# Linear attention's chunks with four tiles of its output gate between them, its result transposed after the fourth and fifth product of the first mixing, two first weights in pages

## The chip, the core and the metric

The program runs on one core of a Trainium2 chip. The metric is device time in microseconds (us) of one execution, from start to end of the whole layer; lower is better. Engines of the core run side by side and each works its own queue of instructions in order: TensorE (PE, matmuls and transposes), VectorE (DVE), ScalarE (ACT), GpSimd (POOL) and SyncE (SP, which here only issues transfers).

## What is computed

One layer of a streaming encoder on 1024 tokens of width 1024 in float32: four token mixers read one projection of the normed stream, each is mapped to the model's width, weighed by a gate and added up; a gated feed-forward block follows. The change lies in the fourth mixer, gated linear attention (4 heads, 64 key and 128 value columns each, chunks of 64 tokens), and in the step that maps a mixer's result to the model's width.

```python
def gla_mixer(q, k, v, g_lr, og, w_g2, b_g, o_norm):
    ...
    q_in = qc * jnp.exp(bcum)
    k_in = kc * jnp.exp(-bcum)
    k_st = kc * jnp.exp(b_last - bcum)
    tri = jnp.tril(jnp.ones((CHUNK, CHUNK), dtype=bool))
    att = jnp.where(tri, jnp.einsum('cbhtd,cbhsd->cbhts', q_in, k_in), 0.0)
    o_intra = jnp.einsum('cbhts,cbhsv->cbhtv', att, vc)
    ...
    def step(state, inp):
        q_c, k_c, v_c, d_c = inp
        o_c = jnp.einsum('bhtd,bhdv->bhtv', q_c, state)
        state = d_c[..., None] * state + jnp.einsum('bhtd,bhtv->bhdv', k_c, v_c)
        return state, o_c
    ...
    o = rms_norm(o, o_norm.reshape(GLA_HEADS, GLA_DV)).reshape(bsz, seq, GLA_VW)
    return o.astype(dt) * jax.nn.silu(og)

# in reference():
        o = jnp.stack([o_a, o_b, o_c, o_d], axis=2)
        br = jnp.einsum('bskc,kcd->bskd', o, w_branch[l])
        g = jax.nn.sigmoid(gate).reshape(bsz, seq, N_BRANCH, D_MODEL)
        mixed = jnp.sum(g * br, axis=2) @ w_out[l]
```

## The kernel before

**Exactness and tiles.** A float32 product is made of three passes in a faster format: each operand is split into a high and a low part (`split`: ACT copies the high part, DVE subtracts it to get the low one), and PE multiplies high by high, high by low and low by high. So `fm` and `tm` issue three matmuls for each block of 128 inner columns. A page is a tile of 128 partitions by 1024 numbers. Weights come through three small rings: `wr` (raw, as loaded by SP, 2 buffers), `wh` and `wl` (high and low, 3 buffers each). A raw buffer is loaded again once the split of its content has been issued and is done; a split buffer is written again once its matmuls are done. Accumulators in PSUM are also rings: `ps` has 3 buffers of 1024 columns, `p1` has 2 of 512.

**Linear attention, `gla()`.** Two pairs of heads (p = 0, 1), 8 blocks of 128 tokens, that is 2 chunks each (i). `factors()` has earlier stored six pages for each pair in DRAM: the decayed queries and keys, and `qb0`, `qb1`, which hold the queries of one head with zeros in place of the other. `gla()` loads them again as `gl` (12 pages, some of them early), then `vd`, the values, 4 pages. `within(p, i)` multiplies keys by queries into one `ps` buffer, and DVE masks the result into `att`. `across(p, i)` multiplies queries by the running state, `att` by the values, and keys by the values for the next state (`po`, a `p1` buffer); DVE updates the state, ACT copies the result into `od` (4 pages). The loop runs `within` two steps ahead of `across`. These products are plain float32 matmuls, which the trace shows as two rows for each call.

**The output gate, `gla_out_gate`.** For each of 8 token tiles: 24 matmuls of 512 columns with the weights `wog`, then Silu on ACT into `og`. In the kernel before, tiles 0 to 3 are called ahead of the loop and tiles 4 to 7 after it; the tile scheduler moves the first `within` steps between them. After the loop `norm` works on each page of `od`: Square on ACT (`sq`), a sum on DVE (L811), two small operations on POOL (`rsqrt`, L284 and L285), a multiplication on DVE (L815). `og` is multiplied by `o_norm` (DVE, L827), and `finish()` multiplies `od` by `og` (DVE, 8 pieces of 512 columns, L835) and transposes `od` on PE (32 transposes into 4 `ps` buffers, L846), copies them (`odt`, ACT) and stores them for a later mixing.

**Mixing, `mixing(k)`.** `o` holds the split result of mixer k, transposed (8 pages, from `load_o`, which loads `oraw` and splits it). For each of 8 blocks m of 128 output columns: load a weight (`wr`, 128 by 512) and the gate (`g`), split the weight, 24 matmuls into one `ps` buffer, and a DVE multiplication of that by `g` into `acc` (L893, called the evacuation of m below). Mixing 0 follows `gla()` at once. `bg` is a queue of steps that are put between (`tick`): the norms in `gla_out_gate`, then `finish()` and the loads of the next `o` (`load_o(1, h)`) between the blocks m.

The order of instructions on each engine in this part is the tile scheduler's: it is decided when the program is built and fixed in each queue. Each engine's queue is strictly in order, and so a waiting instruction holds up all behind it. In the listings below a name such as `ps_763_5420` is a buffer's name with its number, and "x2" are two instructions alike.

Of the kernel before, what the change touches and what calls it, by code (L numbers as in the profile page):

```python
# [11 lines left out]
F32R = mybir.dt.float32r  # L12
I32 = mybir.dt.int32
AF = mybir.ActivationFunctionType
# [3 lines left out]
P = 128  # L18
# [59 lines left out]
class Trunk:  # L78
# [155 lines left out]
        return prev  # L234

    SPEC = {"wb": (4, P, 4)}

    def pre(self, name, idx):

# [408 lines left out]
    def factors(self):  # L648
# [14 lines left out]
        ps = self.psum()  # L663
# [28 lines left out]
        for p in range(2):  # L692
# [35 lines left out]
            ps = self.psum()  # L728
            for i in range(NT):
                nc.tensor.transpose(ps[:, i * P:(i + 1) * P], ks2[:, i * P:(i + 1) * P], self.ident)  # L730
            qb = [self.page("qb") for _ in range(2)]
            for h in range(2):
                r, z = slice(h * 64, h * 64 + 64), slice(64 - h * 64, 128 - h * 64)
                nc.gpsimd.memset(qb[h][z, :], 0.0)
                nc.vector.tensor_copy(out=qb[h][r, :], in_=b[r, :])
                nc.gpsimd.dma_start(out=self.glo[p][3 + h], in_=qb[h])
            yield
            kt = self.page("kt")
            nc.scalar.copy(out=kt, in_=ps)
# [6 lines left out]
    def gla(self):  # L746
# [13 lines left out]
            qs, ki, ks, qb0, qb1, kt = (self.gl[p][j] for j in range(6))  # L760
            io[p] = qs, ki, ks, (qb0, qb1), kt, self.dec2[p]
        vd = [self.fetched_page(self.vds[j], "vd") for j in range(4)]
        self.gla_out_gate(range(0, 4), og, 0)

        od = [[self.page("od") for _ in range(2)] for p in range(2)]

        def within(p, i):
            qs, ki, ks, qb, kt, dec2 = io[p]
            tok = slice(i * P, (i + 1) * P)
            pa = self.psum()  # L770
            for h in range(2):
                nc.tensor.matmul(pa[:, h * P:(h + 1) * P], ki[:, tok], qb[h][:, tok], start=True, stop=True)
            for h in range(2):
                nc.tensor.matmul(pa[:, 256 + h * P:256 + (h + 1) * P], ks[:, tok], qb[h][:, tok], start=True, stop=True)
            t = att[2 * p + i % 2]
            nc.vector.copy_predicated(out=t, mask=self.tri, data=pa[:, 0:256])
            t3 = t.rearrange("p (h t) -> p h t", h=2)
            nc.vector.tensor_copy(out=t3[0:64, :, 64:128], in_=pa[0:64, 256:512].rearrange("p (h t) -> p h t", h=2)[:, :, 64:128])

        def across(p, i):  # L780
            qs, ki, ks, qb, kt, dec2 = io[p]
# [14 lines left out]
            nc.scalar.copy(out=od[p][i // 4][:, (i % 4) * 256:(i % 4) * 256 + 256], in_=po[:, 0:256])  # L796

        seq = [(p, i) for i in range(NT) for p in range(2)]
        within(*seq[0])
        within(*seq[1])  # L800
        for j, it in enumerate(seq):
            if j + 2 < len(seq):
                within(*seq[j + 2])
            across(*it)

        def norm(p, j):
# [14 lines left out]
        for h in range(4):  # L821
            for _ in self.load_o(0, h):
                pass
        self.gla_out_gate(range(4, 8), og, 2)
        for j in range(4):
            o3 = og[j].rearrange("p (b c) -> p b c", b=2)
            nc.vector.tensor_mul(out=o3, in0=o3, in1=go[:, 0:512].unsqueeze(1).to_broadcast([P, 2, 512]))  # L827
# [9 lines left out]
        def finish():  # L837
            for p in range(2):
                for j in range(2):
                    gate(p, j)  # L840
                    yield
            for p in range(2):
                for h in range(2):
                    ps = self.psum()
                    for i in range(NT):
                        nc.tensor.transpose(ps[:, i * P:(i + 1) * P], od[p][i // 4][:, (i % 4) * 256 + h * P:(i % 4) * 256 + (h + 1) * P], self.ident)  # L846
                    yield
                    o = self.page("odt")
                    nc.scalar.copy(out=o, in_=ps)
                    nc.gpsimd.dma_start(out=self.spill[3][2 * p + h], in_=o)  # L850
        self.bg.append(finish())

    def gla_out_gate(self, tiles_, og, n):
        for i in tiles_:
# [14 lines left out]
    def mixing(self, k, last=False, then=None):  # L869

        nc, a = self.nc, self.a
        o, self.o = self.o, []
        self.pre("wb", 8 * k)
        if then is not None:
            self.bg.extend(self.load_o(then, h) for h in range(4))

        def fetch(m):
            g = self.page("g")
            nc.sync.dma_start(out=g, in_=self.fmo[16 + 8 * k + m])
            return g  # L880

        nxt = fetch(0)
        for m in range(8):
            g = nxt
            if m + 1 < 8:
                self.pre("wb", 8 * k + m + 1)
                nxt = fetch(m + 1)
            self.tick(2)
            ps = self.psum()
            self.fm(ps, self.w("wb", 8 * k + m), o)  # L890
            if self.acc[m] is None:
                self.acc[m] = self.page("acc")
                nc.vector.tensor_mul(out=self.acc[m], in0=ps, in1=g)  # L893
            else:
                nc.vector.tensor_mul(out=g, in0=ps, in1=g)
                nc.vector.tensor_add(out=self.acc[m], in0=self.acc[m], in1=g)
            if last:
                nc.gpsimd.dma_start(out=self.accs[m], in_=self.acc[m])
# [61 lines left out]
    def latent(self):  # L960
# [7 lines left out]
        for i in range(NT):  # L968
            ps = self.psum1()
            self.tm(ps[:, 0:336], self.hrows(i), w)  # L970
            nc.scalar.copy(out=q_at(i, 0, 336), in_=ps[:, 0:336])
        w = self.weights(a["wc"][1], 8, 336, 3)
        sk, sq = self.small(8), self.small(8)
        junk = self.page("junk")
        for i in range(NT):
# [621 lines left out]
    def run(self):  # L1597
# [18 lines left out]
        with ExitStack() as e1:  # L1616
            self.psp = e1.enter_context(tc.tile_pool(name="psum", **big))
            with ExitStack() as e2:
# [2 lines left out]
                self.hl = hp.tile([P, 8, S], F32R, name="hl")  # L1621
                self.columns(self.ranks(self.gmlp()))
                self.o = []
                self.gla()
                for h in range(4):
                    self.dump(f"oa{h}", self.spill[0][h])
                    self.dump(f"ob{h}", self.spill[1][h])
                self.mixing(0, then=1)
                self.drain()
                for h in range(4):  # L1630
                    self.dump(f"od{h}", self.spill[3][h])
# [113 lines left out]
```

## Time and profile before

| | |
|---|---|
| median of 3 runs | 1917.24 us (1915.26 to 1917.99) |
| profiled execution, its own time | 1917.36 us |
| its span, first to last instruction | 1915.6 us |
| PE busy | 1871.1 us (98%), 9000 matmuls recorded |
| DVE / ACT / POOL busy | 65% / 45% / 11% |
| chain that ended last | PE 85%, DVE 6%, ACT, DMA, POOL and issue 2% each |
| mean granted clock of TensorE | 0.997 |

PE is busy nearly all the time, and the chain of work that ended last runs mostly through it. So a change can gain by less work on PE or by fewer of its few waits, and lose by a new wait. A profile row of a matmul states when it started and how long it took; matmuls overlap, so that the distance between starts is what one costs. The part that the change touches lies between 600 and 740 us.

### The profile page before, as it was taken

Reading aid. Unit: us, or ns where it says so; the run is one execution under the profiler, and the core shown is the slowest. Engines: PE = TensorE matmul, PEld = TensorE weight load, DVE = VectorE, ACT = ScalarE, POOL = GpSimd, SP = SyncE. Lnnn points to the kernel's source line nnn. Section 1 sums busy time; section 2 is a strip of 40 time slices with the busy share of each in tenths; the row PEclk is TensorE's granted clock in tenths of the full one; section 3 lists DMA queues with packets and bytes.
Section 4 is the critical chain, followed back from the end, with each engine's and each line's share of the span. In section 5 each row is a group of like instructions: output and inputs, shape, how many; then the busy total and the mean of one; then the engine's idle time right before and its main releaser. Section 6 shows DMA issues by size and latency. Waiting matters only on the chain.

```text
span 1915.6 us, 23556 instructions
## 1 busy us (share of the span) xinstructions
PE 1871.1 (98%) x9000; PEld 1562.5 (82%) x9000; DVE 1254.6 (65%) x1752; ACT 861.4 (45%) x1304; POOL 205.9 (11%) x357
## 2 busy tenths in 40 slices
PE   7999999999999999999999999999999999999998
PEld 6988888887887878988788788788888888888887
DVE  5757676664773557436888872687777777774652
ACT  5433465535453221242777633364444444442431
POOL 2000000010110020021122200300000000000101
PEclk9999999999999999999999999999999999999999
DMA  6123344372556335245000353213333323686651
GB/s 220 50 88 132 132 151 153 137 254 99 204 214 231 115 118 206 67 134 177 16 23 29 144 205 130 99 45 131 111 110 110 113 107 115 229 311 212 254 186 44
DMA packets 88289, 268.60 MB, mean 140 GB/s; under 512 B 9488, under 2 KB 15392, under 8 KB 88176
## 3 DMA queue, kind: packets, MB, share of 16 engines
q1 hardware_dynamic: 58896, 174.68, 26.9%
q0 software_dynamic: 21664, 78.45, 10.3%
q10 hardware_dynamic: 7616, 13.96, 2.3%
q8 instruction: 71, 1.16, 0.2%
q14 instruction: 42, 0.34, 0.1%
HBM read 186.78 MB, written 80.28 MB: 139 GB/s over the span
## 4 chain that ended last, share of the span: by engine, by line
PE 85%; DVE 6%; issue 2%; ACT 2%; DMA 2%; POOL 2%; SPq 0%; DVEq 0%; ACTq 0%; POOLq 0%
PE bk L167 22%; PE ps L167 16%; PE bk L1533 12%; PE p L277 9%; PE ps L268 7%; PE p L167 6%; PE ps L277 2%; PE ps L1081 2%; PE po L1132 2%; PE p L1266 2%; PE pp L1117 1%; POOL sm L285 1%; DVE ang L953 1%; DVE wl L123 1%; DMA gl<-gl 1%
## 5 line engine op out<-in xcount | busy, mean ns | idle before, releaser
L1533 PE MATMUL bk<-dh,g 128*128 128x512 f32 x704 | 217.1, 389 | 0.2 <-DVE q L1544 0.2
L167 PE MATMUL bk<-q,wh 128*128 128x512 f32 x704 | 216.7, 389 | 0.0
L122 ACT CAST wh<-t 128x1024 fp32r<-128x1024 f32 x85 | 89.5, 1053 | 273.4 <-PE bk L167 123.2
L123 DVE TENSOR_TENSOR wl<-wr,wh 128x1024 fp32r<-128x1024 f32 (+7 forms) x107 | 103.4, 968 | 117.9 <-ACT wh L122 116.9
L167 PE MATMUL ps<-S,wh 128*128 128x512 f32 x560 | 173.2, 390 | 1.3 <-ACT zb L216 1.3
L1533 PEld LDWEIGHTS bk<-dh,g 128*128 128x128 f32 x704 | 132.2, 188 | 28.1 <-DVE q L1544 0.6
L167 PEld LDWEIGHTS bk<-q,wh 128*128 128x128 f32 x704 | 132.2, 188 | 27.4
L122 ACT CAST wh<-wr 128x1024 fp32r<-128x1024 f32 (+7 forms) x107 | 90.4, 847 | 136.1 <-PE ps L268 67.5
L268 PE MATMUL ps<-o,wh 128*128 128x512 f32 x512 | 139.9, 394 | 3.8 <-ACT o L122 1.5
L1533 PE MATMUL bk<-dl,g 128*128 128x512 f32 x352 | 137.0, 389 | 0.0
L167 PE MATMUL bk<-q,wl 128*128 128x512 f32 x352 | 136.9, 389 | 0.0
L167 PEld LDWEIGHTS ps<-S,wh 128*128 128x128 f32 x560 | 104.8, 188 | 23.5 <-ACT zb L216 2.0
L123 DVE TENSOR_TENSOR wl<-t,wh 128x1024 fp32r<-128x1024 f32 x85 | 103.8, 1221 | 28.8 <-ACT wh L122 28.7
L268 PEld LDWEIGHTS ps<-o,wh 128*128 128x128 f32 x512 | 95.6, 189 | 25.9 <-DVE o L123 2.8
L167 PE MATMUL ps<-S,wl 128*128 128x512 f32 x280 | 109.0, 389 | 0.0
L167 PE MATMUL bk<-S,wh 128*128 128x512 f32 x304 | 93.6, 389 | 0.0
L123 DVE TENSOR_TENSOR dl<-dr,dh 128x1024 fp32r<-128x1024 f32 x44 | 53.7, 1221 | 45.5 <-ACT dh L122 38.7
L268 PE MATMUL ps<-o,wl 128*128 128x512 f32 x256 | 79.4, 393 | 3.0 <-DVE wl L123 3.0
L167 PEld LDWEIGHTS bk<-q,wl 128*128 128x128 f32 x352 | 66.1, 188 | 13.7
L1533 PEld LDWEIGHTS bk<-dl,g 128*128 128x128 f32 x352 | 66.1, 188 | 13.6
L167 PE MATMUL p<-hh,wh 128*128 128x512 f32 x184 | 72.5, 394 | 0.4 <-ACT za L206 0.4
L167 PE MATMUL p<-hh,wl 128*128 128x512 f32 x184 | 71.9, 391 | 0.9 <-DVE wl L123 0.9
(459 smaller groups left out, 4414.4 us busy)
## 6 DMA issues: line engine op xcount, KB each, us to landing
wr<-in_wf SPq DMA_DIRECT2D x48, 512.0 KB, 4.2
wr<-in_up SPq DMA_DIRECT2D x44, 512.0 KB, 3.6
dr<-in_down SPq DMA_DIRECT2D x44, 512.0 KB, 5.2
g<-fm SPq DMA_DIRECT2D x32, 512.0 KB, 5.8
fm<-za POOLq DMA_DIRECT2D x22, 512.0 KB, 2.9
fm<-zb POOLq DMA_DIRECT2D x22, 512.0 KB, 2.9
ga<-fy POOLq DMA_DIRECT2D x22, 512.0 KB, 2.9
gb<-fy POOLq DMA_DIRECT2D x22, 512.0 KB, 2.9
```

Source lines behind the costliest of these rows:

```text
L122: self.nc.scalar.copy(out=hi, in_=src)
L123: self.nc.vector.tensor_sub(out=lo, in0=src, in1=hi.bitcast(F32))
L167: self.nc.tensor.matmul(ps, l[:, c], r, start=first and k == 0 and j == 0, stop=last and k == 3 and j == 2, skip_group_check=True)
L268: self.nc.tensor.matmul(ps[:, h * 512:(h + 1) * 512], lhs, rhs[:, h * 512:(h + 1) * 512], start=first and k == 0 and j == 0, stop=last and ...
L277: self.nc.tensor.matmul(ps, lhs, rhs, start=first and k == 0 and j == 0, stop=last and k == K - 1 and j == 2)
L285: nc.gpsimd.tensor_tensor(out=r, in0=t, in1=self.mhalf[:, 0:w], op=ALU.pow)
L953: nc.vector.scalar_tensor_tensor(out=ang, in0=t, scalar=-c, in1=ang, op0=ALU.mult, op1=ALU.add)
L1081: nc.tensor.matmul(ps[:, off + c0:off + c1], l[:, q0], r[:, c0:c1], start=jj == 0, stop=jj == 2)
L1117: nc.tensor.transpose(pp[:, at:at + P], probs[u][j][0][:, kb * P:(kb + 1) * P], self.ident)
L1132: nc.tensor.matmul(po[:, c], vs[2 * m + kk][:, head * P:(head + 1) * P], ptt[:, z * 512 + kk * 256:z * 512 + kk * 256 + c.stop - c.start], ...
L1266: self.nc.tensor.matmul(ps, l, x, start=k == 0 and j == 0, stop=k == K - 1 and j == 2)
L1533: nc.tensor.matmul(ps, l, r[:, halves[c]], start=first and n == 0 and j == 0, stop=last and n == len(gs) - 1 and j == 2)
```

## The change

1. `factors()` writes the queries in another layout: each page now holds both heads of 4 token blocks side by side. It takes four DVE copies and four POOL memsets of half the size in place of two and two.
2. `within()` makes one matmul of 256 columns for both heads in place of two of 128, and one of 128 columns with 64 weight columns in place of two of 128 by 128.
3. The output gate's tiles 2 to 5 are issued in groups of six matmuls between the steps of the loop, into `ps` buffers; tiles 0 and 1 stay ahead of the loop, 6 and 7 follow it. In `gla()` SP's queue now has the order in which the code issues its loads.
4. The weights of the first block of mixing 0 and of mixing 3 are loaded and split in pages of their own (`pre_page`), not in the rings. All later weights of mixing 0 thereby move one place in the rings.
5. The transposes of `od` (`turned`) are taken out of `finish()` and go into `bg` behind the four loads of the next `o`.

```diff
+    def pre_page(self, idx):
+        raw, t = self.page("pwr")[:, 0:512], self.page("pwt", F32R)
+        self.nc.sync.dma_start(out=raw, in_=self.a["wb"][idx])
+        self.split(raw, t[:, 0:512], t[:, 512:1024])
+        self.fetched["wb", idx] = [(t[:, j * P:(j + 1) * P], t[:, 512 + j * P:512 + (j + 1) * P]) for j in range(4)]
...
-            qb = [self.page("qb") for _ in range(2)]
-            for h in range(2):
-                r, z = slice(h * 64, h * 64 + 64), slice(64 - h * 64, 128 - h * 64)
-                nc.gpsimd.memset(qb[h][z, :], 0.0)
-                nc.vector.tensor_copy(out=qb[h][r, :], in_=b[r, :])
-                nc.gpsimd.dma_start(out=self.glo[p][3 + h], in_=qb[h])
+            for n in range(2):
+                qb = self.page("qb")
+                q4 = qb.rearrange("p (i h t) -> p i h t", h=2, t=P)
+                for h in range(2):
+                    r, z = slice(h * 64, h * 64 + 64), slice(64 - h * 64, 128 - h * 64)
+                    nc.gpsimd.memset(q4[z, :, h, :], 0.0)
+                    nc.vector.tensor_copy(out=q4[r, :, h, :], in_=b[r, n * 512:(n + 1) * 512].rearrange("p (i t) -> p i t", t=P))
+                nc.gpsimd.dma_start(out=self.glo[p][3 + n], in_=qb)
...
-        self.gla_out_gate(range(0, 4), og, 0)
+        self.gla_out_gate(range(0, 2), og, 0)
...
-            for h in range(2):
-                nc.tensor.matmul(pa[:, h * P:(h + 1) * P], ki[:, tok], qb[h][:, tok], start=True, stop=True)
-            for h in range(2):
-                nc.tensor.matmul(pa[:, 256 + h * P:256 + (h + 1) * P], ks[:, tok], qb[h][:, tok], start=True, stop=True)
+            q = qb[i // 4][:, (i % 4) * 256:(i % 4) * 256 + 256]
+            nc.tensor.matmul(pa[:, 0:256], ki[:, tok], q, start=True, stop=True)
+            nc.tensor.matmul(pa[0:64, 256:384], ks[:, i * P:i * P + 64], q.rearrange("p (h t) -> p h t", h=2)[:, :, 64:128], start=True, stop=True)
...
+        def parts():
+            for i in range(2, 6):
+                ps, l = self.psum()[:, 0:512], self.hrows(i)
+                for c in range(0, 8, 2):
+                    self.tm(ps, l[c:c + 2], self.wog[c:c + 2], first=c == 0, last=c == 6)
+                    if c < 6:
+                        yield
+                nc.scalar.activation(out=og[i // 2][:, (i % 2) * 512:(i % 2) * 512 + 512], in_=ps, func=AF.Silu)
+                yield
+        fill = parts()
...
             if j + 2 < len(seq):
                 within(*seq[j + 2])
+            next(fill, None)
             across(*it)
...
-        self.gla_out_gate(range(4, 8), og, 2)
+        self.pre_page(0)
+        self.gla_out_gate(range(6, 8), og, 4)
...
+        def turned():
             for p in range(2):
                 for h in range(2):
                     ps = self.psum()
...
-        self.pre("wb", 8 * k)
+        if ("wb", 8 * k) not in self.fetched:
+            self.pre("wb", 8 * k)
         if then is not None:
-            self.bg.extend(self.load_o(then, h) for h in range(4))
+            self.bg.extend(self.load_o(then[0], h) for h in range(4))
+            self.bg.append(then[1])
...
+        self.pre_page(24)
...
-                self.gla()
+                with self.tc.manual_schedule(engines={mybir.EngineType.SP}):
+                    turned = self.gla()
...
-                self.mixing(0, then=1)
+                self.mixing(0, then=(1, turned))
```

How the queues change is shown at two places. **The end of the norms.** Before, DVE's queue has these instructions up to the first evacuation of mixing 0, L893, the last row here (L815 is a norm's multiplication, L827 `og` by `o_norm`, L835 `od` by `og`, L123 the low part of a weight):

```order
L815 TENSOR_TENSOR od_662_4891<-od_662_4891,sm_722_5250 128x1024
L815 TENSOR_TENSOR od_663_4892<-od_663_4892,sm_727_5285 128x1024
L827 TENSOR_TENSOR og_643_4760<-og_643_4760,go_639_4755 128x1024
L123 TENSOR_TENSOR wl_730_5295<-wr_728_5293,wh_729_5294 128x512
L123 TENSOR_TENSOR wl_734_5303<-wr_732_5301,wh_733_5302 128x512
L835 TENSOR_TENSOR od_661_4890<-od_661_4890,og_643_4760 128x512
L835 TENSOR_TENSOR od_662_4891<-od_662_4891,og_640_4757 128x512
L835 TENSOR_TENSOR od_662_4891<-od_662_4891,og_641_4758 128x512
L835 TENSOR_TENSOR od_663_4892<-od_663_4892,og_642_4759 128x512
L835 TENSOR_TENSOR od_663_4892<-od_663_4892,og_643_4760 128x512
L123 TENSOR_TENSOR wl_740_5342<-wr_738_5340,wh_739_5341 128x512
L893 TENSOR_TENSOR acc_737_5338<-ps_736_5313,g_731_5299 128x1024
```

In the changed kernel DVE's queue has there (L834 is a norm's sum; L838, L851 and L859 are its multiplication, `og` by `o_norm` and `od` by `og`; L922 is the evacuation of block m0 out of `ps_735`):

```order
L838 TENSOR_TENSOR od_658_4847<-od_658_4847,sm_716_5215 128x1024
L838 TENSOR_TENSOR od_659_4848<-od_659_4848,sm_720_5224 128x1024
L834 TENSOR_REDUCE sm_723_5256<-sq_722_5254 128x8
L851 TENSOR_TENSOR og_643_4770<-og_643_4770,go_639_4765 128x1024
L838 TENSOR_TENSOR od_660_4849<-od_660_4849,sm_725_5259 128x1024
L834 TENSOR_REDUCE sm_727_5265<-sq_726_5263 128x8
L859 TENSOR_TENSOR od_658_4847<-od_658_4847,og_640_4767 128x512
L838 TENSOR_TENSOR od_661_4850<-od_661_4850,sm_729_5268 128x1024
L859 TENSOR_TENSOR od_658_4847<-od_658_4847,og_641_4768 128x512
L859 TENSOR_TENSOR od_659_4848<-od_659_4848,og_642_4769 128x512
L859 TENSOR_TENSOR od_659_4848<-od_659_4848,og_643_4770 128x512
L922 TENSOR_TENSOR acc_736_5316<-ps_735_5291,g_730_5277 128x1024
```

In both the evacuation stands behind the last norm. In the changed kernel the weights' low parts come ahead of all four norms, two sums ahead of the first row here, and the four products with `og` directly ahead of the evacuation. PE's queue in the changed kernel, in the third block of mixing 0 (`ps_751` is block m2, `ps_763` is m3; m0 was `ps_735` and m1 `ps_741`):

```order
L275 MATMUL ps_751_5373<-o_699_5157,wh_738_5319 128x512 x2
L275 MATMUL ps_751_5373<-o_700_5158,wh_738_5319 128x512 x2
L275 MATMUL ps_763_5420<-o_699_5157,wh_744_5358 128x512 x2
L275 MATMUL ps_763_5420<-o_700_5158,wh_744_5358 128x512
L275 MATMUL ps_751_5373<-o_699_5157,wl_739_5320 128x512 x2
L275 MATMUL ps_751_5373<-o_702_5163,wh_738_5319 128x512 x2
L275 MATMUL ps_751_5373<-o_703_5164,wh_738_5319 128x512 x2
L275 MATMUL ps_751_5373<-o_702_5163,wl_739_5320 128x512 x2
```

Before, all 24 matmuls of a block stand together from m2 on, with transposes between m1 and m2:

```order
L268 MATMUL ps_742_5352<-o_706_5145,wh_733_5302 128x512 x2
L268 MATMUL ps_742_5352<-o_707_5146,wh_733_5302 128x512 x2
L268 MATMUL ps_742_5352<-o_706_5145,wl_734_5303 128x512 x2
L846 MATMUL ps_748_5387<-cst_72,od_661_4890 128x128 x2
L846 MATMUL ps_750_5399<-cst_72,od_660_4889 128x128 x4
L846 MATMUL ps_750_5399<-cst_72,od_661_4890 128x128 x4
L268 MATMUL ps_751_5408<-o_697_5127,wh_739_5341 128x512 x2
L268 MATMUL ps_751_5408<-o_698_5128,wh_739_5341 128x512 x2
```

So after four matmuls of m2, PE's queue now has three of m3, whose `ps` buffer is that of m0; before, blocks m0 and m1 were mixed in this way.

**Around the evacuation of m3.** Before, DVE's queue (`acc_762` is the evacuation of m3, `acc_773` that of m4):

```order
L123 TENSOR_TENSOR wl_765_5496<-wr_763_5494,wh_764_5495 128x512
L893 TENSOR_TENSOR acc_762_5492<-ps_761_5467,g_747_5385 128x1024
L123 TENSOR_TENSOR wl_776_5542<-wr_774_5540,wh_775_5541 128x512
L123 TENSOR_TENSOR o_770_5508<-oraw_768_5505,o_769_5507 128x1024
L893 TENSOR_TENSOR acc_773_5538<-ps_772_5513,g_756_5441 128x1024
```

In the changed kernel (`acc_764` is the evacuation of m3, `wl_778` is the low part of the weight of m6, the `o` pages are those of mixing 1):

```order
L123 TENSOR_TENSOR wl_767_5449<-wr_765_5447,wh_766_5448 128x512
L123 TENSOR_TENSOR wl_778_5509<-wr_776_5507,wh_777_5508 128x512
L123 TENSOR_TENSOR o_758_5409<-oraw_750_5371,o_757_5408 128x1024
L123 TENSOR_TENSOR o_761_5415<-oraw_759_5412,o_760_5414 128x1024
L922 TENSOR_TENSOR acc_764_5445<-ps_763_5420,g_746_5363 128x1024
```

The evacuation of m3 now stands behind two weights and two pages of the next `o`. SP's queue before:

```order
L131 DMA wr_774_5540<-in_wb 128x512
L879 DMA g_756_5441<-fm20_119 128x1024
L131 DMA wr_786_5587<-in_wb 128x512
L879 DMA g_766_5500<-fm21_120 128x1024
L545 DMA oraw_768_5505<-spill1_0_87 128x1024
L131 DMA wr_799_5680<-in_wb 128x512
L545 DMA oraw_771_5511<-spill1_1_88 128x1024
```

SP's queue in the changed kernel:

```order
L131 DMA wr_776_5507<-in_wb 128x512
L552 DMA oraw_750_5371<-spill1_1_88 128x1024
L908 DMA g_756_5406<-fm20_119 128x1024
L131 DMA wr_786_5566<-in_wb 128x512
L131 DMA wr_798_5658<-in_wb 128x512
L552 DMA oraw_759_5412<-spill1_2_89 128x1024
L552 DMA oraw_762_5418<-spill1_3_90 128x1024
```

The load `oraw_759`, from which `o_761` is made, now stands behind `wr_798`, whose raw buffer is that of `wr_776`, the weight that `wl_778` is made of. On PE the transposes into `ps_771` and `ps_773` now stand directly behind m3, and m4 (`ps_774`) behind these, in the buffer of m3.

## Rows read from the trace of the kernel before

**Rows 1.** Waits of PE, 612 to 700 us: total, times, longest.

```profile
PE ps L268 <- DVE wl L123: 3.0, 1, 3.0
PE p L787 <- issue: 1.4, 1, 1.4
PE ps L774 <- DMA gl<-gl: 1.0, 1, 1.0
PE ps L772 <- DVE att L778: 0.8, 1, 0.8
PE ps L772 <- DMA gl<-gl: 0.5, 1, 0.5
PE p L787 <- ACT od L796: 0.4, 1, 0.4
```

**Rows 2.** Timeline of PE in one step of the loop: start, duration, instructions.

```profile
644.00 0.61 PE L772 MATMUL ps<-gl,gl 128*128 128x128 f32 x4
...
644.88 0.60 PE L787 MATMUL p<-state,gl 128*128 128x256 f32 x2
...
646.20 0.61 PE L772 MATMUL ps<-gl,gl 128*128 128x128 f32 x4
```

**Rows 3.** Chain that ended last, the gate's last three tiles: start, length.

```profile
664.19 16.38 PE p L277 x72
```

**Rows 4.** Windows of PE: window, length, busy (instructions), granted clock, DMA share, GB/s.

```profile
691.48:694.21 2.73, 2.73 (x7) 0.50 0.59 188
...
614.00:623.00 9.00, 6.62 (x53) 1.00 1.02 411
```

**Rows 5.** Timeline of PE at the start of mixing 0.

```profile
691.48 1.22 PE L268 MATMUL ps<-o,wl 128*128 128x512 f32 x2 [3.02 <-DVE wl L123]
692.50 1.91 PE L268 MATMUL ps<-o,wh 128*128 128x512 f32 x4
694.21 0.67 PE L268 MATMUL ps<-o,wl 128*128 128x512 f32 x2
```

**Rows 6.** Timeline of ACT in the norms: start, duration of the whole row.

```profile
670.20 2.00 ACT L809 ACTIVATE sq<-od 128x1024 f32<-128x1024 f32 x2
...
682.98 1.13 ACT L122 CAST wh<-wr 128x512 fp32r<-128x512 f32 x2
```

**Rows 7.** Timeline of DVE in the norms.

```profile
671.29 2.35 DVE L811 TENSOR_REDUCE sm<-sq 128x8 f32<-128x1024 f32 x2 [3.35 <-ACT sq L809]
674.59 1.22 DVE L815 TENSOR_TENSOR od<-od,sm 128x1024 f32<-128x1024 f32 x1 [0.95 <-POOL sm L285]
677.63 1.23 DVE L815 TENSOR_TENSOR od<-od,sm 128x1024 f32<-128x1024 f32 x1 [1.82 <-POOL sm L285]
...
679.91 1.89 DVE L835 TENSOR_TENSOR od<-od,og 128x512 f32<-128x512 f32 x3
```

**Rows 8.** Timeline of POOL in the norms.

```profile
672.61 0.19 POOL L284 TENSOR_SCALAR sm<-sm 128x8 f32<-128x8 f32 x1 [62.41 <-DVE sm L811]
...
674.63 1.23 POOL L284 TENSOR_SCALAR sm<-sm 128x8 f32<-128x8 f32 x1
```

**Rows 9.** Timeline of DVE in mixing 0, a page of the next `o`.

```profile
723.59 0.68 DVE L123 TENSOR_TENSOR wl<-wr,wh 128x512 fp32r<-128x512 f32 x1
...
730.50 1.23 DVE L123 TENSOR_TENSOR o<-oraw,o 128x1024 fp32r<-128x1024 f32 x1 [1.73 <-ACT o L122]
731.65 1.22 DVE L893 TENSOR_TENSOR acc<-ps,g 128x1024 f32<-128x1024 f32 x1
```

**Rows 10.** Timeline of PE, transposes between two blocks of mixing 0.

```profile
709.08 1.03 PE L846 MATMUL ps<-cst,od 128*128 128x128 f32 x8
```

**Rows 11.** Instructions on the tile `vd`: its loads, issue to landing.

```profile
L545 SPq DMA_DIRECT2D vd<-vd x4: 319/319/448, 612.1 to 619.7; - x4
...
DMA to landing us min/median/max: 2.9/7.4/15.2
```

**Rows 12.** Instructions on the tile `oraw`, 600 to 760 us: issue to landing.

```profile
DMA to landing us min/median/max: 3.4/4.7/11.4
```

More of the change, by code (lines that the diff above doesn't have):

```diff
@@ L777, in within @@
             t3 = t.rearrange("p (h t) -> p h t", h=2)
-            nc.vector.tensor_copy(out=t3[0:64, :, 64:128], in_=pa[0:64, 256:512].rearrange("p (h t) -> p h t", h=2)[:, :, 64:128])
+            nc.vector.tensor_copy(out=t3[0:64, :, 64:128], in_=pa[0:64, 256:384].rearrange("p (h t) -> p h t", h=2))
         def across(p, i):
@@ L851, in gla @@
         self.bg.append(finish())
+        return turned()
     def gla_out_gate(self, tiles_, og, n):
```

## The prediction

> **What bounds the kernel now.** The chain that ended last was read first: it runs mostly through PE, whose matmuls follow one another without a gap nearly everywhere. So only work on PE and its waits count. PE's waits between 612 and 700 us came next [rows 1]: in the loop's region (614 to 664) they add up to 0.5 + 1.0 + 0.8 + 1.4 + 0.4 = 4.1 us, for `gl` pages, for `att`, for the state and for `od`. The longest, 3.0 us, is at the start of mixing 0, where PE stands before `wl`: on DVE that split is queued behind the last norm. Then the timelines of PE and of the engines it waits for, the windows for the clock, and for what is new the queues of the changed kernel, as the part on the change shows them.
>
> **Part 1: `within` gets narrower.** In a steady step the four calls of `within` (two rows each in the trace) start at 644.00 and the next product at 644.88, so they cost 0.88 us for 512 columns [rows 2]. A whole step takes 646.20 - 644.00 = 2.20. The new pair has 256 and 128 columns, three quarters: 0.66. I take that the time goes with the columns; that half the weight columns of the second call are left out gives nothing more. Sixteen steps by 0.22: -3.5 us. If only the number of calls counted, it would be half, 0.44 by 16 = -7.0; if the narrow call cost as much as two, 0.
>
> **Part 2: the gate's tiles between the steps.** The work is the same; a group of six matmuls costs 6 x 16.38/72 = 1.36 us [rows 3]. What could be gained are the loop's waits. But what they wait for stays late. `vd` is issued from 612.1 on and its first page lands up to 15.2 later, at 627.3 [rows 11]. PE leaves gate tile 1 at 614.0; the first steps of `within` (six at 0.66), gate tile 2 (5.5) and a wait of 1.5 to 2 for the page of `gl` that ended the old wait of 1.0 bring it to the first `across` at about 625.3: it waits some 2.0 us for `vd`, which in the kernel before gate tiles 2 and 3 covered. With some 0.4 for copies of `od` the new waits are 1.7 + 2.0 + 0.4 = 4.1, against 4.1; I book -0.2, with bounds of -3 (transfers a little earlier) and +2.
>
> **Part 3: the start of mixing 0.** Its first weight lies in a page, split while gate tile 7 runs, and its `o` pages are done: the wait of 3.0 goes: -3.0. After it the clock was at its lower level: from 691.48 to 694.21, 2.73 us, six matmuls ran at a granted clock of 0.50 [rows 4, 5], that is 1.2 GHz; at full speed they take 1.36. So another -1.4. The small waits of transposes for a copy go at one place and come at another: 0.
>
> **Part 4: what stands before PE next.** I count from C, the end of the loop. Gate tiles 6 and 7 are 48 matmuls, 10.9 us [rows 3]. Then PE has m0 (24 matmuls), m1 (24) and four of m2, and then three of m3, in the `ps` buffer of m0. So 100 matmuls after C, at C + 22.75, it needs the evacuation of m0. On DVE that stands behind the whole of the norms, and these begin late: ACT's first instruction of this stretch is the split of `wr` for m1, into a `wh` buffer that PE gives back in gate tile 7, after its sixth matmul: 30 matmuls, C + 6.8, and 0.2 to the signal. Behind it in ACT's queue wait a second cast and a Silu, about half a us each (1.13 for two casts), and the first Square, 1.0 [rows 6]: the first sum starts at about C + 9.6.
>
> From there DVE's own pace in the trace: sum to first multiplication 674.59 - 671.29 = 3.3, to the second 677.63 - 674.59 = 3.0 [rows 7]: C + 12.9 and C + 15.9. The third sum follows after 1.1 and its multiplication 3.3 later, C + 20.4; the fourth sum and multiplication likewise, C + 24.8. Then its own 1.1, three products with `og` (1.89), C + 27.8, and the evacuation, 1.2: C + 29.0. PE waits 29.0 - 22.75 = 6.3 us. POOL's first operation can make it more: it took 0.19 alone and 1.23 when a DVE multiplication ran beside it [rows 8]; in the third and fourth norm `og` by `o_norm` and a product run beside it, so up to 1.0 more each: 8.3. I take 7.0, nearer to the lower end, since the product is only half as long as a multiplication.
>
> The Trainium skill, GPSIMD Engine Reference, section 1 (Specifications), says that GpSimd shares its SBUF interface with VectorE and is held up by DVE instructions with two SBUF inputs. The trace agrees with it (0.19 against 1.23); by that rule each norm would pay, and the wait would be 8.3.
>
> **Part 5: the evacuation of m3.** Let E be the end of m3. PE has 16 transposes behind it, 1.03 for 8 [rows 10], about 2.0 us, and then m4, whose `ps` buffer is that of m3. On DVE that evacuation stands behind `wl_778` (its `wh` waits for PE's end of m3), and `o_761`. `o_761` is made of `oraw_759`, which SP issues behind `wr_798`, which waits for `wl_778`. The same chain of split, raw load, page load, its split and evacuation stands in the trace: from `wl` at 723.59 to the end of `acc` at 731.65 + 1.22, 9.3 us [rows 9]. There three buffers of `ps` gave it time. Here it starts at about E + 0.7 (the cast of `wh`) and ends at E + 10.0; PE is there at E + 2.0 and waits 8.0. A page lands in 3.4 at the least, and 4.7 in the median [rows 12], which sets the lower bound 1.3 lower, 6.7. I take 7.5.
>
> **The clock after the new waits.** A wait of 3.0 cost 1.4 after it, and in 614 to 623, with shorter waits, the clock stayed at 1.00 [rows 4]. The two new waits are longer than 3.0, so I book 1.4 for each, +2.8, with bounds of 0 and 3.4 (1.7 each). The Trainium skill, TensorE: Matmul & The Clock Gate, section "Why this matters for your kernels", advises against idle gaps between bursts of matmuls, since the clock returns to its low level. The trace agrees at 691.48; by that rule the change, which brings two such gaps, pays for both.
>
> **Edits at no cost.** The new layout of the queries moves the same number of elements in two more copies and two more memsets for each pair; it lies beside the long run of matmuls ahead of 600 us, where DVE and POOL have time; without that cover it would be four more starts, below 2 us. The page for mixing 3's first weight: that mixing waits for its `o` pages in the trace, not for a weight, so 0; a first weight has cost at most 3.0 [rows 1], so -3.0 is the other bound.
>
> **The sum.** -3.5 - 0.2 - 3.0 - 1.4 + 7.0 + 7.5 + 2.8 = +9.2 us. The profiled execution took 1917.36, 0.1 above the median: 1917.3 + 9.2 = 1926.5.
>
> **The rivals.**
> - *One wait only* (0.12). If `oraw_759` is in time, since the first wait lets the loads run ahead, or if the norms keep pace, one of the two remains: -8.1 + 7.2 + 1.4 = +0.5, 1917.8. For it speaks that a wait at m3 delays PE but not the loads before it; against it, that `wr_798` hangs on E itself, whenever that comes.
> - *No wait at all* (0.10), the other side. The evacuations come in time if the norms end 6.3 us earlier than worked out, which takes Squares that begin at C + 2 and not at C + 8.6, and if m3's evacuation hangs on no load. Then -8.1 is left: 1909.2. It decides as soon as waits and clock together stay under 4.3. For it: the Square of the first pages has its input long before C. Against it: ACT's queue, in which the cast for m1 stands ahead.
> - *The loop waits too* (0.06). If `vd` or the last `gl` page lands 2 us later, now uncovered by gate tiles, PE waits 2 more in two places and the clock falls once (1.4): 1926.5 + 3.4 = 1929.9.
>
> **How the numbers follow.** The two waits (0.72) have a range of their own: the least sum is -8.1 + 6.3 + 6.7 + 0 = +4.9, the most -8.1 + 8.3 + 8.0 + 3.4 = +11.6, so 1922 to 1929. The range reaches from the case of one wait to that of the loop, 1917.3 to 1930, and leaves out the case without waits and little else. 0.2%, 3.8 us, is about what a measurement of this kernel can tell from no change. Slower by over that: 0.72 + 0.06 = 0.78; within it, one wait: 0.12; faster: 0.10.
>
> **What the profile of the changed kernel would show.** Two waits of PE in mixing 0, some 12 us after its start and again behind the transposes after m3, each released by an evacuation on DVE and each followed by a clock of 0.5 (parts 4, 5); no wait at its start and the clock at full there (part 3); steps of the loop of 2.0 us without their gate group (part 1); a wait of about 2 us ahead of the first `across`, released by `vd` (part 2). The prediction is wrong if DVE reaches the evacuation of m0 within 22.75 us of C, or if the load behind `wr_798` lands before PE has done the transposes.

## The result and the profile after

The changed kernel took 1929.6 us in the median of 3 runs (1929.53 to 1932.64) against 1917.24: a ratio of 1.0073, 95% interval 1.0059 to 1.0086. By the ratio that is 14 us, by the medians 12.4; 9.2 had been forecast, and 1930.0 was the upper end of the range. The profiled execution is the one of 1932.64 (span 1930.9), 3 us above the other two; that part lies elsewhere, at 1105 us (below).

The page's chain that ended last, by engine:

```profile
PE 81%; issue 7%; DVE 5%; ACT 2%; POOL 2%; DMA 2%; SPq 0%; POOLq 0%; DVEq 0%; ACTq 0%
```

PE has 81% of it where it had 85%, and "issue", time for which the profile shows no cause, 7% where it had 2%. PE's waits from 600 to 760 us (total, times, longest) show where, as [rows 1] do for the kernel before:

```profile
PE ps L275 <- DVE acc L922: 14.5, 2, 7.6
PE ps L784 <- DMA gl<-gl: 0.7, 1, 0.7
PE p L797 <- issue: 0.5, 1, 0.5
PE ps L782 <- DMA gl<-gl: 0.4, 1, 0.4
...
PE p L797 <- ACT od L806: 0.2, 1, 0.2
```

The 3.0 for `wl` is gone and the loop's waits have shrunk from 4.1 to 1.8 us, but two waits for an evacuation stand in mixing 0, 14.5 us together. The windows of PE (length, busy, granted clock, DMA share, GB/s), from the first `within` to the start of mixing 0, then the two waits and what followed each of them:

```profile
613.42:683.79 70.37, 68.58 (x329) 1.00 0.33 124
...
695.74:703.36 7.62, 0.00 (x1) 0.70 0.00 0
703.36:708.99 5.63, 5.63 (x13) 0.50 0.66 234
...
718.01:724.88 6.87, 0.00 (x0) 0.84 0.95 342
724.88:729.47 4.59, 4.58 (x11) 0.50 0.28 116
```

The first wait lasts 7.62 us and the clock is at 0.50, 1.2 GHz, for 5.63 us behind it; the second 6.87, and 4.59 behind it. At 1.2 GHz half of such a stretch is lost: 2.8 and 2.3 us. The stretch ahead of mixing 0 took 70.37 us; before it was 685.83 - 613.96 = 71.87, so 1.5 were gained where 3.7 had been expected.

A step of the loop in PE's timeline, to be read against [rows 2]:

```profile
635.10 0.59 PE L782 MATMUL ps<-gl,gl 128*128 128x256 f32 x2
635.63 0.43 PE L784 MATMUL ps<-gl,gl 128*64 128x128 f32 x2
635.99 0.50 PE L284 MATMUL ps<-wh,hh 128*128 128x512 f32 x1
636.33 0.39 PE L284 MATMUL ps<-wl,hh 128*128 128x512 f32 x1
...
637.49 0.59 PE L797 MATMUL p<-state,gl 128*128 128x256 f32 x2
...
638.79 0.59 PE L782 MATMUL ps<-gl,gl 128*128 128x256 f32 x2
```

The pair of `within` runs from 635.10 to 635.99, 0.89 us, as long as the four calls before. The gate's six matmuls take 637.49 - 635.99 = 1.50 where 1.36 had been booked, and the first of them takes 0.34 to the next, the others 0.23. The whole step is 3.69 us (635.10 to 638.79); a step of before with a group would be 2.20 + 1.36 = 3.56.

The chain ahead of the first wait's end (start, length; nine of its rows):

```profile
680.44 0.61 ACT pwt L122
681.05 0.49 ACT og L884
681.55 0.96 ACT sq L832
...
682.53 1.23 DVE sm L834
...
684.12 1.67 POOL sm L292
685.87 1.24 POOL sm L291
...
690.01 1.22 DVE sm L834
...
695.39 1.14 DVE sm L834
...
701.98 1.24 DVE acc L922
```

It is that of part 4: the cast of the page, Silu, Square, the sums, each norm a turn through POOL, and the evacuation at 701.98. POOL's two small operations, four times each, are 9.7 of the 22.8 us from 680.44 to the evacuation's end, more than any other engine's share; no run here moves them to another engine. The chain ahead of the second wait's end:

```profile
715.84 0.63 ACT wh L122
...
716.49 0.70 DVE wl L123
...
717.21 0.33 SPq L131
...
717.60 3.69 DMA oraw<-spill
...
721.30 1.05 ACT o L122
...
723.52 1.23 DVE acc L922
```

That is part 5: `wh` at the end of m3, `wl`, the raw load of `wr`, the load of a page behind it in SP's queue (3.69 us), its split, and the evacuation. Two waits more were not foreseen. One is in the stage of the latent attention. The second stands at 1105 us, with 3.4 us of low clock behind it; the times of the other two runs, 3 us shorter, suggest that they do not have it:

```profile
PE sp L1296 <- DVE g L924: 1.4, 1, 1.4
```

```profile
PE ps L275 <- ACT o L122: 1.7, 1, 1.7
```

### The profile page after: what moved, and what is told of

Same layout as the page of the kernel before. It is cut to its first block, busy times and chain, and to the rows that moved or that the text cites. A ratio compares the mean times of both kernels' runs of the same rounds, so it can differ in the third digit from the quotient of the medians.

```text
span 1930.9 us, 23437 instructions
## 1 busy us (share of the span) xinstructions
PE 1874.8 (97%) x8936; PEld 1557.5 (81%) x8936; DVE 1254.8 (65%) x1756; ACT 860.1 (45%) x1304; POOL 205.1 (11%) x361
## 4 chain that ended last, share of the span: by engine, by line
PE 81%; issue 7%; DVE 5%; ACT 2%; POOL 2%; DMA 2%; SPq 0%; POOLq 0%; DVEq 0%; ACTq 0%
PE bk L167 22%; PE bk L1563 12%; PE ps L167 12%; PE ps L275 9%; PE p L284 8%; PE p L167 5%; PE ps L284 4%; PE ps L1111 2%; PE po L1162 2%; PE p L1296 1%; PE pp L1147 1%; POOL sm L292 1%; POOL sm L291 1%; DMA oraw<-spill 1%; DMA gl<-gl 1%
## 5 line engine op out<-in xcount | busy, mean ns | idle before, releaser
L123 DVE TENSOR_TENSOR wl<-wr,wh 128x1024 fp32r<-128x1024 f32 (+7 forms) x105 | 101.5, 969 | 122.4 <-ACT wh L122 121.5
L275 PE MATMUL ps<-o,wh 128*128 128x512 f32 x480 | 134.7, 401 | 16.8 <-DVE acc L922 14.5
L123 DVE TENSOR_TENSOR wl<-t,wh 128x1024 fp32r<-128x1024 f32 x85 | 103.7, 1220 | 28.7 <-ACT wh L122 28.7
L123 DVE TENSOR_TENSOR dl<-dr,dh 128x1024 fp32r<-128x1024 f32 x44 | 53.7, 1221 | 44.0 <-ACT dh L122 37.0
L275 PE MATMUL ps<-o,wl 128*128 128x512 f32 x240 | 75.5, 397 | 0.0
```

What stands on the lines that cost most here:

```text
L123: self.nc.vector.tensor_sub(out=lo, in0=src, in1=hi.bitcast(F32))
L275: self.nc.tensor.matmul(ps[:, h * 512:(h + 1) * 512], lhs, rhs[:, h * 512:(h + 1) * 512], start=first and k == 0 and j == 0, stop=last and ...
```

## The experiments

Each expectation was written before its kernel ran. Each kernel's time stands beside runs of the kernel before on the same chip (median 1917.2 in the first four, 1916.4 in the next, 1916.0 in the last), and the ratios are to these.

**x1, x2: the narrow products alone.** x1 is the kernel before with the new layout of the queries and this:

```diff
+            nc.tensor.matmul(pa[:, 0:256], ki[:, tok], q, start=True, stop=True)
+            nc.tensor.matmul(pa[0:64, 256:384], ks[:, i * P:i * P + 64], q...[:, :, 64:128], start=True, stop=True)
```

x2 differs from x1 in the second call:

```diff
+            nc.tensor.matmul(pa[:, 256:384], ks[:, tok], q...[:, :, 64:128], start=True, stop=True)
```

x1: 

> The kernel before with the new layout of the queries and the narrower pair of products in the loop alone (256 columns, and 128 columns with 64 weight columns); everything else as before. Prediction's term (time goes with the columns): a step of the loop 2.20 - 0.22 = 1.98 us, the loop 3.5 us shorter, time 1913.5 to 1914. Rival, from the trace of the changed kernel (635.10 to 635.99 for the pair, 0.89): the 64-column weights cost what the columns save, step 2.20, time 1917 within 1. Second rival: the pair costs 0.66 here, and the 0.23 more in the changed kernel is what the gate's matmuls behind it pay.

x2: 

> As the first, but the second product keeps 128 weight columns (128 partitions out, of which 64 are read). If 64 weight columns are what cost: step 1.98 us, loop 3.5 shorter, time near 1913.7. If the cost is one of calls or of the mixed widths and not of the 64 columns: the same as the first run. By the prediction's term alone both runs are alike at 1.98.

x1 took 1919.3 us, ratio 1.0012 (1.0003 to 1.0021), above both times that had been expected, part of it by the clock behind the old wait; x2 took 1915.6, 0.9996 (0.9986 to 1.0006). A step in PE's timeline of x1, and then of x2:

```profile
650.21 0.59 PE L774 MATMUL ps<-gl,gl 128*128 128x256 f32 x2
650.74 0.43 PE L776 MATMUL ps<-gl,gl 128*64 128x128 f32 x2
651.10 0.70 PE L789 MATMUL p<-state,gl 128*128 128x256 f32 x2
651.63 0.61 PE L791 MATMUL p<-vd,att 128*128 128x128 f32 x4
...
652.51 0.59 PE L774 MATMUL ps<-gl,gl 128*128 128x256 f32 x2
```

```profile
650.37 0.59 PE L774 MATMUL ps<-gl,gl 128*128 128x256 f32 x2
650.80 0.39 PE L776 MATMUL ps<-gl,gl 128*128 128x128 f32 x2
651.02 0.60 PE L789 MATMUL p<-state,gl 128*128 128x256 f32 x2
651.45 0.61 PE L791 MATMUL p<-vd,att 128*128 128x128 f32 x4
...
652.33 0.59 PE L774 MATMUL ps<-gl,gl 128*128 128x256 f32 x2
```

In x1 the pair takes 0.89 (650.21 to 651.10), and the product with the state behind it 0.53 instead of 0.44; a step is 2.30 us, longer than the 2.20 before. In x2 the pair takes 0.65 and a step 1.96. So the time does go with the columns, and the 64 weight columns cost it back, by 0.34 us in each step. The Trainium skill, TensorEngine Tiling (Array Packing), section "Key Properties", says that TensorE is drained when the tiling mode changes. The 0.34 us would fit such a change at the 64-column call, the only one that differs between x1 and x2; that this call changes the mode, or that there is a drain, no run here shows. x2 is 16 x 0.24 = 3.8 us shorter in its steps, but gave 1.6 in its median: in its profile PE waits 1.7 for `gl` and 0.9 for `att` ahead of 621.2, and the clock is low for 3.3 us behind that.

**x3: the gate's tiles between the steps alone.** The kernel before with this and with SP in code order:

```diff
-        self.gla_out_gate(range(0, 4), og, 0)
+        self.gla_out_gate(range(0, 2), og, 0)
...
+            next(fill, None)
             across(*it)
...
-        self.gla_out_gate(range(4, 8), og, 2)
+        self.gla_out_gate(range(6, 8), og, 4)
```

> The kernel before with the gate's tiles 2 to 5 between the steps of the loop and the loads of that part in code order alone; four calls in each step as before, mixing as before. Prediction's term: -0.2 us in all, work between the steps costs nothing of its own. Rival: each change from plain float32 matmuls to split ones costs 0.11 us (in the trace of before 623.40 to 623.72 is 0.32 where others are 0.227), 16 changes, +1.6, less the old loop's waits that go (4.1 to about 1.8): -0.7. The wait at the start of mixing 0 stays near 3.0 with its clock loss. Time 1915 to 1918.

It took 1922.3, ratio 1.0025 (1.0014 to 1.0036): above both expectations. Its longest wait, and a group of the gate behind four calls of 128 columns, in PE's timeline:

```profile
PE ps L268 <- DVE wl L123: 9.0, 1, 9.0
```

```profile
648.40 0.47 PE L277 MATMUL ps<-wh,hh 128*128 128x512 f32 x1
648.72 0.39 PE L277 MATMUL ps<-wl,hh 128*128 128x512 f32 x1
...
649.87 0.59 PE L787 MATMUL p<-state,gl 128*128 128x256 f32 x2
...
651.18 0.61 PE L772 MATMUL ps<-gl,gl 128*128 128x128 f32 x4
...
651.99 0.47 PE L277 MATMUL ps<-wh,hh 128*128 128x512 f32 x1
```

The wait at the start of mixing 0 has grown from 3.0 to 9.0. With two gate tiles left behind the loop, and not four, the norms have 10.9 us less cover; in the kernel before, the first two norms ran beside tiles 5 and 6 [rows 7]. The wait grew by less than 10.9, since `wl` stands behind three multiplications of norms in x3's DVE queue (it starts at 694.80) and behind four in that of before.

A group takes 1.47 here and its first matmul 0.32 to the next, but the four calls ahead of it take 0.81 (651.18 to 651.99) and not 0.88. The step is 3.59 (648.40 to 651.99), and 2.20 + 1.36 = 3.56: the change from plain to split matmuls costs some 0.03 us in a step, not the rival's 0.11. From the first `within` to the start of mixing 0 x3 takes 69.55 us, 2.3 less than before, as much as the loop's waits have lost (4.1 to 1.8).

**x4: the changed kernel with the transposes early again.**

```diff
-        def turned():
             for p in range(2):
...
-        return turned()
+        return iter(())
```

> The changed kernel with the transposes back among the first blocks of mixing 0 as in the kernel before; all else as changed. Prediction's parts 4 and 5: the wait for the evacuation of m3 (6.9 measured) goes with the low clock behind it (2.3); the first wait of about 7.6 stays, now at the transposes or at the block behind them, since the norms are as late as they were: 1929.6 - 9.2 = 1920 within 1.5. Rival: the two waits have one cause, the late norms; then the second stays at 5 or more in another place and the time stays above 1926.

It took 1919.2, ratio 1.0010 (1.0000 to 1.0019), as expected. The second wait is gone; the first has moved to the transposes and is 6.1 us:

```profile
PE ps L870 <- DVE od L859: 5.5, 2, 3.2
PE ps L870 <- DVE acc L920: 0.6, 1, 0.6
```

**x5: the waits filled.** The changed kernel with 35 and 28 matmuls more, ahead of m2 and of m4, whose result nobody reads:

```diff
+            if k == 0 and m in (2, 4):
+                self.idle(o, 35 if m == 2 else 28)
             self.fm(ps, ww, o)
```

> The changed kernel with 35 matmuls more ahead of block m2 and 28 more ahead of m4 of mixing 0, on operands that are there already, into a buffer that nobody reads: 63 by 0.227 = 14.3 us of work in place of the 14.5 us that PE waits. If the low clock behind the two waits comes from PE standing still, it stays at full speed and some 5 us come back although PE has more to do: 1924 to 1926. If the clock fell for another reason (the time since the start, what DVE does), the time stays at 1929.6. If the evacuations are late because PE's own blocks are late, the waits stay and the time rises to 1940 or more.

It took 1925.8, ratio 1.0043 (1.0028 to 1.0058), inside the expected range and 3.8 us faster than the changed kernel, with 14.3 us more work on PE. The windows of PE:

```profile
600.00:700.00 100.00, 98.63 (x461) 1.00 0.35 130
700.00:740.00 40.00, 39.15 (x187) 1.00 0.58 208
```

The clock stays at 1.00, and of the two waits 0.3 us is left. From the start of mixing 0 to the transposes behind m4 this trace takes 44.4 us (683.70 to 728.05) and that of the changed kernel 48.8 (683.79 to 732.60). So the low clock came from PE standing still, and it cost nearly what the windows of the changed kernel say (5.1).

**x6: the transposes last, alone.** The kernel before with `turned` behind the four loads.

```diff
+            self.bg.append(then[1])
```

> The kernel before with the transposes alone put behind the loads of the next mixer's result, as in the change; loop, gate and weights as before. Prediction's part 5: the wait for the evacuation of m3 hangs on the load behind a raw weight and comes without the first wait: 6.7 to 8.0 us at m4 and about 2.3 of low clock, 1917.2 + 9 = 1926, 1924 to 1928. Rival: it comes only because the late norms push everything: then no wait over 2 us at m4 and 1916 to 1919.

It took 1919.4, ratio 1.0014 (1.0004 to 1.0023), far below the 1924 to 1928 of the prediction's term and just above the rival's upper end:

```profile
PE ps L268 <- DVE wl L123: 3.7, 1, 3.7
PE ps L268 <- DVE acc L897: 2.5, 1, 2.5
```

The wait for the evacuation of m3 is there, but 2.5 us long. SP's queue differs from that of the changed kernel: the load of that page stands ahead of the last raw weight, not behind it, and was issued at 710.30, 2.8 us ahead of the end of m3 (713.08). So the late transposes alone bring 2.5 us; the rest of the 6.9 needs a load that comes late as well, here by its place in the queue.

**x7: x2 with the first weight of mixing 0 in a page.**

```diff
+        self.pre_page(0)
         self.gla_out_gate(range(4, 8), og, 2)
```

> The kernel before with the narrower products in the form with 128 weight columns and the first weight of mixing 0 in a page; gate and transposes as before. Prediction's part 3: the wait of 3.0 and the 1.4 of low clock behind it go: 1915.6 - 4.4 = 1911.2, 1910 to 1912.5. Rival: the transposes of the first blocks then wait for the products with the gate, as they did in the run with the transposes early (5.5 there), and take 2 or 3 us back: 1913 to 1915.5.

It took 1912.9, ratio 0.9982 (0.9972 to 0.9991). The wait of 3.0 is gone, and one of 2.3 for the evacuation of m0, behind the norms, has come, so that the time lies between the two expectations:

```profile
PE ps L275 <- DVE acc L904: 2.3, 1, 2.3
```

**x8: the changed kernel with 128 weight columns.** The edit of x2.

> The changed kernel with 128 weight columns in the second product of the loop's step. In the trace of the changed kernel the pair took 0.89 and a group of the gate behind it 1.50 instead of 1.36; if both come from the 64 columns, a step falls from 3.69 to about 3.40 us, the loop by 4.5, and the time to 1925 within 1.5; the two waits in mixing 0 stay at 7.6 and 6.9. Rival: the change between plain and split matmuls is what costs; then the step falls by 0.1 or less and the time stays above 1928.

It took 1927.2, ratio 1.0049 (1.0032 to 1.0065), 0.7 above the expected range. The step fell as expected, to 3.35 us. From the first `within` to the start of mixing 0 it took 66.6 us, 3.8 less than in the changed kernel, but 2.4 is what the median shows: the two waits grew from 14.5 to 15.4, and one of 0.6 for `vd` came.

**x9: the changed kernel with two of four norms in the loop.**

```diff
+            if j in (9, 11, 12, 13, 14, 15):
+                if j == 9:
+                    self.bg.extend(norm(p, 0) for p in range(2))
+                self.tick()
```

> The changed kernel with the norms of the first two pages of the result (token blocks 0 to 3) issued inside the loop's second half, where these pages are already complete; two norms are left for after the loop. Prediction's part 4 (the norms, begun too late, hold up the evacuation of m0): with two of the four gone from the chain after the loop, the evacuation of m0 comes at about C + 20.7, ahead of PE's C + 22.75; the wait of 7.6 and its low clock of 2.8 go. The scheduler then puts the load from which the second wait hangs ahead of the last raw weight, so that this wait falls too, to about the 2.5 of the run with the transposes last: 1929.6 - 10.4 - 4.4 - 1 = 1914, 1912 to 1920. Rival: the wait is set by the transfers or the weights' splits and not by the norms; then a wait of 5 or more stays ahead of m3 and the time is above 1923.

It took 1917.0, ratio 1.0004 (0.9994 to 1.0014). The first wait is gone, so it was the norms. The second stayed at 5.5, where 2.5 had been expected: its load, now ahead of the last raw weight, took 7.1 us, as the chain shows. So a place ahead of that weight is not enough; the page has to land in time. Why it took 7.1 us, and 3.7 in the changed kernel, is open.

```profile
PE ps L275 <- DVE acc L925: 5.5, 1, 5.5
```

```profile
704.03 7.12 DMA oraw<-spill
```

**x10: the changed kernel with the next mixer's loads ahead.**

```diff
+            raws = [self.fetched_page(self.spill[then[0]][h], "oraw") for h in range(4)]
...
```

> The changed kernel with the four loads of the next mixer's result issued at the start of mixing 0, ahead of the raw weights; their splits and the transposes stay in their places. Prediction's part 5 (the evacuation of m3 hangs on a load behind a raw weight that waits for the end of m3): the wait at m4 falls from 6.9 to under 1 with its low clock of 2.3, the first wait of 7.6 stays: 1929.6 - 9 = 1920.5, 1919 to 1922. Rival: the wait hangs on the splits on ACT and DVE, wherever the load stands: then 4 or more stays at m4 and the time is above 1925.

It took 1920.3, ratio 1.0022 (1.0012 to 1.0031), as expected. One wait is left, and it is the first:

```profile
PE ps L275 <- DVE acc L927: 7.6, 1, 7.6
```

**x11 and x12: the remedies together.** x11 is x7 with the norms of x9; x12 is the changed kernel with x2's columns, x4's transposes and x9's norms.

x11: 

> The kernel of x7 (128 weight columns, the first weight of mixing 0 in a page) with the norms of the first two pages inside the loop. The wait of 2.3 for the evacuation of m0 and the low clock behind it (1.6) go: 1912.9 - 3.9 = 1909, 1908 to 1911. Rival: the norms' work on DVE and ACT in the loop makes across wait for its state, 2 us or more: 1911 to 1913.

x12: 

> The changed kernel with 128 weight columns, the transposes early and the norms of the first two pages inside the loop. From the run with the transposes early (1919.2): -4 for the columns, -6 for the waits of the transposes, -2.5 for their low clock: 1907 to 1911. Against x11 it tells what the gate's tiles between the steps are worth once the waits are gone: by the prediction nothing (0.2); by the trace of x3, 16 changes between plain and split matmuls cost 1.6 and less waiting gives 2.3 back: within 2 us of x11.

x11 took 1911.3, ratio 0.9970 (0.9959 to 0.9981), where its expectation ends and its rival's begins: the wait of 2.3 is gone, and one of 1.0 for the state has come. x12 took 1909.7, 0.9963 (0.9950 to 0.9976). Both beat both kernels, x12 the kernel before by 0.37%, 6 to 7 us. Their intervals overlap: which is the better, and so what the gate's tiles between the steps are worth, isn't settled. The longest waits left in x12 are 1.7 us for `gl` and 1.4 for an evacuation.

## Why the prediction was right in its direction and short in its size

- **Part 1 failed, the largest miss.** "I take that the time goes with the columns; that half the weight columns of the second call are left out gives nothing more": -3.5 was booked. Columns count as assumed (x2), but the 64 weight columns cost 0.34 us in each step, more than the 0.24 saved. A step became 0.10 longer, in x1 (2.30 against 2.20) and in the changed kernel (3.69 against x3's 3.59). Up to mixing 0 the changed kernel took 0.8 us more than x3 (70.37 against 69.55), so that its other bound, 0, did not hold either.
- **Part 2: the work was right, the waits were not.** x3 has this part alone: -2.3 where -0.2 had been booked, within its bounds. The work costs nearly the same (3.59 against 3.56 for a step), but the new waits were 1.8 us and not 4.1. The wait of 2.0 for `vd` did not come: its first page was issued at 612.6 and landed 13.1 later, at 625.7 and not at 627.3, and PE was there at 625.84. That was close: in x8 and x12, whose steps are shorter, PE waits 0.6 and 0.7 for it. Parts 1 and 2 together gave 1.5 in place of 3.7: 2.2 us of the miss.
- **Part 3 was right** for the changed kernel: mixing 0 starts without a wait and at full clock.
- **Parts 4 and 5 were right** in place, chain and size: 7.6 and 6.9 where 7.0 and 7.5 had been booked. That both sums are 14.5 is luck, one being 0.6 short and the other 0.6 over. With C at 672.78, the first sum began at C + 9.75 (9.6 in the prediction) and the evacuation ended at C + 30.4 (29.0, up to 31.0 with POOL). x9 shows for the first wait that the norms are its cause. x4, x6 and x10 show for the second that it takes late transposes and a page that is loaded late; x9, that a load ahead of the last raw weight can still be late. The rival of one wait only fell, and that of no wait at all. The third rival's time, 1929.9, was nearly met, but by chance: the loop waited less and not more.
- **The clock was the other term that failed.** "I book 1.4 for each": it was 2.8 and 2.3, 5.1 in place of 2.8, above the bound of 3.4 as well. The row of before had one wait of 3.0; the low stretch behind the new waits was longer, 5.63 and 4.59 us against 2.73. x5 shows that it came from the waits. One row was too few for a bound: in x1 the same wait of 3.0 had 5.8 us of matmuls at the low clock behind it.
- **"Edits at no cost" missed 1.4 us**, a wait of the latent stage for an evacuation (L924) of the mixing ahead of it. x3, which has no page for mixing 3, has it at the same place, and x4, which has that page, has not. So it is no matter of that page; what decides it stays open.

Term by term the forecast becomes 9.2 + 2.2 + 2.3 + 1.4 = 15.1. Against the kernel before, the profile of the changed one is 0.5 us ahead at 613, lacks a wait of 0.8 at 785 and a low clock at 919.5 (1.4), and has 3.0 more at 1105: 15.4, where the spans differ by 15.3. Without the 3.0, which by their times the other two runs don't have, 12.4 are left, as by the medians; ahead of that place the same matmul starts 12.4 us later in the changed kernel (1099.33 against 1086.92). The time came out at the end of the range and beyond it because the clock's bound and the term for `within` were both too cheap.

## What to carry to other kernels

A step that is freed of its cover must be followed to the next instruction that needs the slowest chain behind it: here the norms lost two gate tiles of cover and the evacuation of the first block, queued behind them, stopped PE. Price a wait on PE with what its clock loses behind it, here 1.4 to 3.0 us after waits of 3 to 9, and price a narrower matmul by its neighbours too: fewer columns of data paid, fewer weight columns cost more than they saved. A load in a queue that is in order should stand ahead of those that wait for the work which it is meant to feed (x10), early enough to land in time (x9).

## What the hardware showed that was not expected

- A matmul with 64 weight columns between those with 128 cost 0.24 us in the pair and 0.10 in the call behind it (x1 against x2).
- The first split matmul behind plain float32 ones takes 0.32 to 0.34 us to the next instead of 0.23 (x3 and the changed kernel), but in x3 the plain ones ahead of it take 0.07 less, so that a step is only 0.03 us longer.
- The low clock held for 2.73 to 6.0 us after matmuls had begun again, and not in step with the length of the wait: behind 3.0 us it was 2.73 in the kernel before and 5.8 in x1, behind 7.6 us 5.63 in the changed kernel and 3.8 in x10, behind 5.5 us 6.0 in x9. Waits of 1.7 and 0.9 had it fall in x2, one of 2.5 in x6 had not. In the kernel before it fell at 919.5 behind waits of 0.7, 1.0 and 0.6 us, and behind the same three in the changed kernel it did not.
